# Longer slots for matmul operands, and one work slot fewer in the attention lane

## The chip, the cores and the metric

The kernel runs on one core of a Trainium2 chip. The metric is the time of one execution on the device in microseconds (us). The profiler records one execution with every instruction of the engines: PE (TensorE's matmuls), PEld (TensorE's weight loads, which run beside the matmuls), DVE (VectorE), ACT (ScalarE), POOL (GpSimd) and SP (SyncE, which issues the transfers here).

## The reference

Two models follow each other on 512 tokens of width 1024. The first has one layer: a mix of gated linear attention, a causal convolution and sliding-window attention, then a feed-forward block of width 2816. The second has two layers, each with attention over the 128 best keys of an index score, a gated recurrence, and a feed-forward block. Cut to the parts that this change touches:

```python
u = rmsnorm(h, g_ffn)                                   # first model
hid = causal_dwconv(u @ w_up, ffn_conv_w)
h = h + (silu(hid[..., :2816]) * hid[..., 2816:]) @ w_down
...
for l in range(2):                                      # second model
    proj = rmsnorm_2(x, norm_mix[l]) @ w_in[l]
    aq, ak, av, iq, ik, iw, hq, hf, hi, hg, ga, gb = split(proj)
    aq, ak = rope(norm(aq)), rope(norm(ak))
    y_attn = dsa_attention(aq, ak, av, rope(iq), rope(ik), iw)   # softmax over top 128 keys
    y_hgrn = norm(hgrn2(hq, hf, hi)) * silu(hg)
    x = x + (sigmoid(ga) * (y_attn @ w_a[l]) + sigmoid(gb) * (y_hgrn @ w_h[l])) @ w_out[l]
    g, u = split(rmsnorm_2(x, norm_ffn[l]) @ w_ffn_in[l])
    x = x + (silu(g) * u) @ w_ffn_out[l]
```

All values are 32-bit floats, and the kernel keeps about that precision.

## The kernel before

Activations lie transposed: eight tiles `h` of 128 features by 512 tokens. Every large product is made of matmuls with a moving operand of 128x512 and a stationary operand of 128x128. To keep precision, each operand is split into a rounded part and a remainder (`xh` and `xl`, `whi` and `wlo`, `acth` and `actl`), and each pair of tiles is multiplied three times: wlo·xh, whi·xl, whi·xh (lines 193 to 195 in `project`). One projection over the model width is eight steps of three matmuls into one bank of the accumulation memory; a down-projection of the feed-forward block has 22 steps. In `project_tokens` (lines 168 to 170) the roles are swapped: 128 columns of `xh` or `xl` are stationary and the weight tile moves, over four token blocks.

`weights` issues the transfer of a raw weight tile from SP (512 KB, one of three `wraw` buffers), lets ACT copy four 128x128 pieces at a time into `whi` and lets DVE or POOL subtract them for `wlo`. There are three `whi` and three `wlo` buffers.

A pool hands out slots. The weight pool holds `wraw`, `whi`, `wlo`; the activation pool holds eight `xh` and eight `xl` (`make_x`); the work pool has the lanes `t` (32 slots: split outputs `acth`, `actl`, `mgh`, `mgl`, the mixes' outputs `yah`, `yhh`, `ych`, `ysh`, `ygh` and their remainders, and other longer-lived tiles), `i` (8), `g` (5), `h` (7, short-lived work of the recurrence and feed-forward) and `a` (7, short-lived work of the attention). Each slot has 512 elements per partition, 2048 bytes. In the built program the slots lie one behind the other, and the first addresses are 54,240 for `whi`, 60,384 for `wlo`, 66,528 for `xh`, 82,912 for `xl` (all 32 above a multiple of 64, and 480 above one of 512) and 115,712 for lane `t` (a multiple of 512).

A scheduler decides the order of instructions on each engine; it knows how many slots each lane has. Each engine then works its list in that order. In a layer of the second model, lane `a` is used by index rotation (`rope`, lines 791 to 794, into `idxr`), score selection (`rel`; DVE's 16 rounds of `max` and `match_replace`, lines 878 and 879), key and query rotation (`rotated`: `rope` into `aro`, a multiplication by the norm on DVE at line 817, four transposes on TensorE at line 239) and attention itself (`aL`, `aPT`, `aon`).

Of the kernel before, what the change touches and what calls it, by code (L numbers as in the profile page):

```python
# [10 lines left out]
F32 = mybir.dt.float32  # L11
F32R = mybir.dt.float32r
# [6 lines left out]
P = 128  # L19
T = 512  # L20
NT = 4
KD = 8
# [26 lines left out]
def constants():  # L49
    c = np.zeros((P, NCST), np.float32)  # L50

    def put(name, a):
        c[:, CST[name][0]:CST[name][1]] = a

    i = np.arange(P)[:, None]
    j = np.arange(P)[None, :]
    put("ident", i == j)
    put("inv", np.float32(10000.0) ** (-np.arange(0, 64, 2, dtype=np.float32) / np.float32(64)))
    k = np.arange(2 * P)[None, :]
    dist = P + i - k  # L60
    put("dist", np.where((dist >= 0) & (dist < P), -dist, NEG))
    put("causal", np.where(j <= i, 0.0, NEG))
    put("unseen", np.where(j <= i, 0.0, UNSEEN))
    m = [(i <= j) & (i // 64 == j // 64), i == j]
    for h in LEVELS:
        n = np.repeat(np.arange(64 // h), h)[None, :]
        m.append((i // (2 * h) == n) & (i % (2 * h) < h))
    return c, np.concatenate(m, axis=1).astype(np.float32)


class Builder:
    def __init__(self, ctx, tc, A):
# [13 lines left out]
        self.mixing()  # L86
        self.pending = None

    def t(self, name, dtype=F32, shape=None):
        return self.bp.tile(shape or [P, T], dtype, name=name, tag="t", bufs=self.SLOTS["t"])  # L90

    SLOTS = {"t": 32, "i": 8, "g": 5, "h": 7, "a": 7}
    BANKS = {"h": 2, "a": 2}

    @contextmanager
# [9 lines left out]
        self.lows = [self.nc.vector]  # L105

    def i(self, name, dtype=F32, shape=None):
        return self.bp.tile(shape or [P, T], dtype, name=name, tag="i", bufs=self.SLOTS["i"])

    def g(self, name, dtype=F32, shape=None):  # L110
        return self.bp.tile(shape or [P, T], dtype, name=name, tag="g", bufs=self.SLOTS["g"])

    def u(self, name, dtype=F32, shape=None):
        return self.bp.tile(shape or [P, T], dtype, name=name, tag="u" + self.lane, bufs=self.SLOTS[self.lane])

# [17 lines left out]
    def weights(self, src, n, w=P, pieces=False):  # L133
        nc = self.nc
        ws = []
        step = 512 // w if w < 512 // 2 else 1
        with self.tc.high_priority():
            raw = self.wp.tile([P, 1024], F32, name="wraw", tag="wraw", bufs=3)[:, 0:n * w].rearrange(
                "p (n w) -> p n w", n=n)
            if pieces:  # L140
                for k in range(n):
                    nc.sync.dma_start(raw[:, k, :], src[:, k, :])
            else:
                nc.sync.dma_start(raw, src)
            for k in range(0, n, step):
                m = min(step, n - k)
                wh, wl = [self.wp.tile([P, 512], F32R, name=a, tag=a, bufs=3)[:, 0:m * w].rearrange(
                    "p (m w) -> p m w", m=m) for a in ("whi", "wlo")]
                nc.scalar.copy(wh, raw[:, k:k + m, :])  # L149
                eng = self.lows[self.count % len(self.lows)]  # L150
                self.count += 1
                eng.tensor_tensor(wl, raw[:, k:k + m, :], wh.bitcast(F32), op=OP.subtract)  # L152
                ws += [(wh[:, i, :], wl[:, i, :]) for i in range(m)]
        return ws

    def project_tokens(self, src, X, out):
        nc = self.nc
        w = src.shape[-1]
        ps = [self.mm() for _ in range(NT)]
        for k in range(0, KD, 2):  # L160
            if k == KD - 2 and self.finish:
                self.finish()
                self.finish = None
            ws = self.first.pop(0) if self.first else self.weights(src[k // 2], 2, w)
            for i, (wh, wl) in zip((k, k + 1), ws):
                for t in range(NT):
                    xh, xl = [x[:, t * P:(t + 1) * P] for x in X[i]]
                    nc.tensor.matmul(ps[t][:, 0:w], xh, wl, start=i == 0, stop=False)  # L168
                    nc.tensor.matmul(ps[t][:, 0:w], xl, wh, start=False, stop=False)  # L169
                    nc.tensor.matmul(ps[t][:, 0:w], xh, wh, start=False, stop=i == KD - 1)  # L170
                    if i == KD - 1:
                        with self.tc.high_priority():
                            out(t, ps[t][:, 0:w], self.rcol[:, t:t + 1])

    def token_copies(self, src, X, name):
        tiles = [self.t(name) for _ in range(NT)]

        def out(t, ps, r):
            self.nc.scalar.activation(tiles[t][:, 0:ps.shape[1]], ps, AF.Copy, scale=r)

        self.project_tokens(src, X, out)
        return tiles
# [53 lines left out]
    def transpose4(self, src, dst, idx=None):  # L236
        ps = self.at([P, NT, P])
        for t in range(NT):
            self.nc.tensor.transpose(ps[:, t, :], src[:, t * P:(t + 1) * P], self.ident)  # L239
        if dst is not None:  # L240
            self.nc.scalar.copy(dst, ps)
        return ps
# [32 lines left out]

    def make_x(self, d, h, g):
        nc = self.nc
        hi = self.xp.tile([P, T], F32R, name="xh", tag="xh", bufs=KD)
        lo = self.xp.tile([P, T], F32R, name="xl", tag="xl", bufs=KD)
        nc.scalar.activation(hi, h, AF.Copy, scale=g)  # L280
        nc.vector.scalar_tensor_tensor(lo, h, g, hi.bitcast(F32), op0=OP.mult, op1=OP.subtract)  # L281
        return hi, lo
# [814 lines left out]
```

## Time and profile before

| | |
|---|---|
| runs | 2606.26, 2607.33, 2609.94 us |
| median | 2607.33 us |
| profiled execution, first to last instruction (span) | 2605.2 us; the profile gives no other time of it |
| TensorE matmuls | busy 2533.9 us, 97% of the span |
| DVE, ACT, POOL | 52%, 38%, 29% |

The span of the profiled execution is 2.1 us under the median of the runs. An engine is busy in a group for as long as at least one of the group's instructions is in flight; successive matmuls overlap in time, so the sum of their durations is more than the busy time, and the rate is read from the distance between starts.

### The profile page before, as it was taken

How to read it: one execution, taken by the hardware profiler on the slowest of the kernel's cores; microseconds unless marked ns; L12 is line 12 of the kernel's file. 1: busy time of each engine (PE TensorE's matmuls, PEld its weight loads, DVE VectorE, ACT ScalarE, POOL GpSimd, SP SyncE). 2: the span in 40 equal slices, each digit the busy share in tenths (PEclk: the TensorE clock that was granted, in tenths of full speed). 3: DMA queues.
4: the chain of work that ended last, by engine and by line, in shares of the span. 5: the costliest groups of instructions: out<-in, count | busy, mean ns of one | idle time of the engine just before them, and what ended most of it. 6: DMA issues, size and time to landing. Idle time of an engine off the chain costs nothing.

```text
span 2605.2 us, 31523 instructions
## 1 busy us (share of the span) xinstructions
PE 2533.9 (97%) x11742; PEld 2040.0 (78%) x11742; DVE 1355.5 (52%) x2568; ACT 1000.8 (38%) x1813; POOL 754.3 (29%) x640
## 2 busy tenths in 40 slices
PE   9999999999999997999999999999799999999999
PEld 7777888788888865777878888887577787888887
DVE  4565322477774579675244444336967524444432
ACT  5543333444443333553343333334354433433321
POOL 4234334511101234443351111013545435211100
PEclk9999999999999999999999999999899999999999
DMA  3112222222222221111322222322110122222232
GB/s 135 57 51 81 93 94 93 101 97 96 97 94 90 90 73 65 42 41 51 99 96 94 97 95 94 96 88 81 65 49 33 45 94 97 97 97 97 95 101 87
DMA packets 67434, 217.66 MB, mean 84 GB/s; under 512 B 7744, under 2 KB 8640, under 8 KB 67280
## 3 DMA queue, kind: packets, MB, share of 16 engines
q1 hardware_dynamic: 67280, 215.65, 24.9%
q8 instruction: 92, 1.51, 0.2%
q14 instruction: 62, 0.51, 0.1%
HBM read 213.52 MB, written 2.10 MB: 83 GB/s over the span
## 4 chain that ended last, share of the span: by engine, by line
PE 83%; DVE 12%; issue 2%; POOL 2%; ACT 1%; DMA 0%; SPq 0%; DVEq 0%; POOLq 0%; ACTq 0%
PE mm L194 24%; PE mm L195 24%; PE mm L193 24%; PE at L917 1%; PE mm L169 1%; PE mm L168 1%; PE mm L170 1%; DVE score L879 1%; PE at L929 1%; DVE m L878 1%; DVE wlo L152 1%; PE at L239 1%; DVE hf L490 1%; DVE rope L792 1%; DVE rsq_w L232 1%
## 5 line engine op out<-in xcount | busy, mean ns | idle before, releaser
L149 ACT CAST whi<-wraw 128x512 fp32r<-128x512 f32 (+3 forms) x824 | 502.2, 610 | 1177.7 <-PE mm L195 992.1
L194 PE MATMUL mm<-xl,whi 128*128 128x512 f32 x1920 | 757.2, 394 | 0.0
L193 PE MATMUL mm<-xh,wlo 128*128 128x512 f32 x1920 | 756.8, 394 | 0.0
L195 PE MATMUL mm<-xh,whi 128*128 128x512 f32 x1920 | 755.5, 393 | 0.0
L152 DVE TENSOR_TENSOR wlo<-wraw,whi 128x512 fp32r<-128x512 f32 (+1 forms) x529 | 387.4, 732 | 457.9 <-ACT whi L149 455.2
L152 POOL TENSOR_TENSOR wlo<-wraw,whi 128x512 fp32r<-128x512 f32 (+2 forms) x295 | 383.6, 1301 | 767.0 <-ACT whi L149 747.1
L194 PEld LDWEIGHTS mm<-xl,whi 128*128 128x128 f32 x1920 | 361.7, 188 | 79.8 <-issue 7.5
L195 PEld LDWEIGHTS mm<-xh,whi 128*128 128x128 f32 x1920 | 361.6, 188 | 78.2 <-issue 5.6
L193 PEld LDWEIGHTS mm<-xh,wlo 128*128 128x128 f32 x1920 | 361.5, 188 | 76.6 <-issue 3.5
L193 PE MATMUL mm<-acth,wlo 128*128 128x512 f32 x528 | 208.6, 395 | 0.0
L195 PE MATMUL mm<-acth,whi 128*128 128x512 f32 x528 | 208.6, 395 | 0.0
L194 PE MATMUL mm<-actl,whi 128*128 128x512 f32 x528 | 208.6, 395 | 0.0
L725 POOL TENSOR_TENSOR fg<-fg,rstd 128x512 f32<-128x512 f32 x44 | 56.7, 1289 | 426.1 <-ACT fg L724 426.1
L168 PE MATMUL mm<-wlo,xh 128*128 128x512 f32 (+2 forms) x384 | 146.6, 382 | 20.0 <-POOL wlo L152 12.4
L170 PE MATMUL mm<-whi,xh 128*128 128x512 f32 (+2 forms) x384 | 144.5, 378 | 0.0
L169 PE MATMUL mm<-whi,xl 128*128 128x512 f32 (+2 forms) x384 | 144.2, 375 | 0.2 <-DVE xl L281 0.2
L202 DVE TENSOR_TENSOR gate<-mm,rstd 128x512 f32<-128x512 f32 x56 | 38.7, 691 | 169.3 <-PE mm L195 169.3
L270 POOL TENSOR_TENSOR acc<-acc,sq 128x512 f32<-128x512 f32 x39 | 58.7, 1506 | 205.9 <-ACT sq L267 204.9
L195 PEld LDWEIGHTS mm<-acth,whi 128*128 128x128 f32 x528 | 99.0, 187 | 24.3
L193 PEld LDWEIGHTS mm<-acth,wlo 128*128 128x128 f32 x528 | 99.0, 187 | 24.2
L194 PEld LDWEIGHTS mm<-actl,whi 128*128 128x128 f32 x528 | 99.0, 187 | 24.2
L168 PEld LDWEIGHTS mm<-wlo,xh 128*128 128x128 f32 x384 | 73.5, 191 | 40.7 <-POOL wlo L152 15.7
(347 smaller groups left out, 3288.3 us busy)
## 6 DMA issues: line engine op xcount, KB each, us to landing
wraw<-in_w_ffn_in SPq DMA_DIRECT2D x88, 512.0 KB, 3.2
wraw<-in_w_gate SPq DMA_DIRECT2D x56, 512.0 KB, 3.2
wraw<-in_w_in SPq DMA_DIRECT2D x52, 512.0 KB, 3.2
wraw<-in_w_up SPq DMA_DIRECT2D x44, 512.0 KB, 3.2
wraw<-in_w_tok SPq DMA_DIRECT2D x32, 512.0 KB, 3.2
wraw<-in_w_ffn_out SPq DMA_DIRECT2D x32, 512.0 KB, 3.5
wraw<-in_w_down SPq DMA_DIRECT2D x16, 512.0 KB, 3.5
wraw<-in_w_po SPq DMA_DIRECT2D x32, 256.0 KB, 2.6
```

The costliest lines, as they stand in the source:

```text
L149: nc.scalar.copy(wh, raw[:, k:k + m, :])
L152: eng.tensor_tensor(wl, raw[:, k:k + m, :], wh.bitcast(F32), op=OP.subtract)
L168: nc.tensor.matmul(ps[t][:, 0:w], xh, wl, start=i == 0, stop=False)
L169: nc.tensor.matmul(ps[t][:, 0:w], xl, wh, start=False, stop=False)
L170: nc.tensor.matmul(ps[t][:, 0:w], xh, wh, start=False, stop=i == KD - 1)
L193: nc.tensor.matmul(ps, wl, xh, start=i == 0, stop=False)
L194: nc.tensor.matmul(ps, wh, xl, start=False, stop=False)
L195: nc.tensor.matmul(ps, wh, xh, start=False, stop=i == n - 1)
L202: self.nc.vector.tensor_tensor(out, ps, other, op=OP.mult)
L232: nc.vector.scalar_tensor_tensor(w, w, -0.5, y, op0=OP.mult, op1=OP.mult)
L270: (nc.vector if d % 2 and len(acc) > 1 else nc.gpsimd).tensor_tensor(a, a, sq, op=OP.add)
L725: nc.gpsimd.tensor_tensor(g, g, self.rstd, op=OP.mult)
```

## The change

Three kinds of buffer become 8 elements, 32 bytes, longer: the work lanes `t`, `i` and `g`, the split weights `whi` and `wlo`, and the split activations `xh` and `xl`. Each tile still uses its first 512 elements. The raw weights, the lanes `h` and `a`, and everything else keep their size. Lane `a` has 6 slots, not 7.

```diff
+    PAD = 8
+
+    def padded(self, pool, name, tag, bufs, dtype=F32, shape=None):
+        a = pool.tile([P, T + self.PAD], dtype, name=name, tag=tag, bufs=bufs)
+        if shape is None:
+            return a[:, 0:T]
+        n = math.prod(shape[1:])
+        if len(shape) == 2:
+            return a[:, 0:n]
+        return a[:, 0:n].rearrange("p (n c) -> p n c", n=shape[1])
+
     def t(self, name, dtype=F32, shape=None):
-        return self.bp.tile(shape or [P, T], dtype, name=name, tag="t", bufs=self.SLOTS["t"])
-
-    SLOTS = {"t": 32, "i": 8, "g": 5, "h": 7, "a": 7}
+        return self.padded(self.bp, name, "t", self.SLOTS["t"], dtype, shape)
+
+    SLOTS = {"t": 32, "i": 8, "g": 5, "h": 7, "a": 6}
...
     def i(self, name, dtype=F32, shape=None):
-        return self.bp.tile(shape or [P, T], dtype, name=name, tag="i", bufs=self.SLOTS["i"])
+        return self.padded(self.bp, name, "i", self.SLOTS["i"], dtype, shape)
 
     def g(self, name, dtype=F32, shape=None):
-        return self.bp.tile(shape or [P, T], dtype, name=name, tag="g", bufs=self.SLOTS["g"])
+        return self.padded(self.bp, name, "g", self.SLOTS["g"], dtype, shape)
...
-                wh, wl = [self.wp.tile([P, 512], F32R, name=a, tag=a, bufs=3)[:, 0:m * w].rearrange(
+                wh, wl = [self.wp.tile([P, 512 + self.PAD], F32R, name=a, tag=a, bufs=3)[:, 0:m * w].rearrange(
...
-        hi = self.xp.tile([P, T], F32R, name="xh", tag="xh", bufs=KD)
-        lo = self.xp.tile([P, T], F32R, name="xl", tag="xl", bufs=KD)
+        hi = self.padded(self.xp, "xh", "xh", KD, F32R)
+        lo = self.padded(self.xp, "xl", "xl", KD, F32R)
```

The addresses in the built program (bytes in each partition; the remainder to 64 in brackets):

| buffer | before | after |
|---|---|---|
| whi | 54240 (32), 56288 (32), 58336 (32) | 54240 (32), 56320 (0), 58400 (32) |
| wlo | 60384 (32), 62432 (32), 64480 (32) | 60480 (0), 62560 (32), 64640 (0) |
| xh | 66528 (32), 68576 (32), ... 80864 (32) | 66720 (32), 68800 (0), ... 81280 (0) |
| xl | 82912 (32), 84960 (32), ... 97248 (32) | 83360 (32), 85440 (0), ... 97920 (0) |
| lane t | 115712 (0), 117760 (0), 119808 (0), ... | 116416 (0), 118496 (32), 120576 (0), ... |

The instructions and their order are the same outside of three places in the attention lane of each layer of the second model; the matmuls of the projections keep their order throughout. The largest of the three places is key rotation. On TensorE, during the token projection of the queries (`whi`, `wlo` against `xh`, `xl`), the four transposes of each rotated key block (`at<-csts,aro`) stood like this before:

```order
L168 MATMUL mm<-wlo,xh 128x512
L169 MATMUL mm<-whi,xl 128x512
L170 MATMUL mm<-whi,xh 128x512
L239 MATMUL at<-csts,aro 128x128 x4
L168 MATMUL mm<-wlo,xh 128x512
L169 MATMUL mm<-whi,xl 128x512
L170 MATMUL mm<-whi,xh 128x512
L239 MATMUL at<-csts,aro 128x128 x4
L168 MATMUL mm<-wlo,xh 128x512
L169 MATMUL mm<-whi,xl 128x512
L239 MATMUL at<-csts,aro 128x128 x4
```

and now:

```order
L181 MATMUL mm<-whi,xh 128x512
L179 MATMUL mm<-wlo,xh 128x512
L180 MATMUL mm<-whi,xl 128x512
L250 MATMUL at<-csts,aro 128x128 x4
L181 MATMUL mm<-whi,xh 128x512
L179 MATMUL mm<-wlo,xh 128x512
L180 MATMUL mm<-whi,xl 128x512
L250 MATMUL at<-csts,aro 128x128 x4
L181 MATMUL mm<-whi,xh 128x512
L179 MATMUL mm<-wlo,xh 128x512
L250 MATMUL at<-csts,aro 128x128 x4
```

The first group of transposes has moved behind two more matmuls; the fourth group, which came three matmuls after the third, now comes fourteen after it. On DVE, in the same place, the norm's multiplication of the rotated keys (`aro<-aro,rsq_y`) stood between the rounds of score selection (`MAX`, `MATCH_REPLACE`) and the last rope product (`rope_8001`) like this before:

```order
L793 TENSOR_TENSOR rope_8001<-akx,tabS 128x8x32
L879 MATCH_REPLACE score<-m_7686,score 128x384
L233 SCALAR_TENSOR_TENSOR rsq_y<-rsq_w,rsq_y 128x32
L878 MAX m_7689<-score 128x8
L817 TENSOR_TENSOR aro<-aro,rsq_y 128x512
L879 MATCH_REPLACE score<-m_7689,score 128x384
L817 TENSOR_TENSOR aro<-aro,rsq_y 128x512
L878 MAX m_7692<-score 128x8
L817 TENSOR_TENSOR aro<-aro,rsq_y 128x512
L879 MATCH_REPLACE score<-m_7692,score 128x384
L817 TENSOR_TENSOR aro<-aro,rsq_y 128x512
```

and now:

```order
L889 MAX m_7689<-score 128x8
L244 SCALAR_TENSOR_TENSOR rsq_y<-rsq_w,rsq_y 128x32
L804 TENSOR_TENSOR rope_8001<-akx,tabS 128x8x32
L890 MATCH_REPLACE score<-m_7689,score 128x384
L828 TENSOR_TENSOR aro<-aro,rsq_y 128x512
L889 MAX m_7692<-score 128x8
L828 TENSOR_TENSOR aro<-aro,rsq_y 128x512
L890 MATCH_REPLACE score<-m_7692,score 128x384
L828 TENSOR_TENSOR aro<-aro,rsq_y 128x512
L889 MAX m_7695<-score 128x8
L889 MAX m_7721<-score 128x8
```

The first multiplication now stands behind the match-replace of `m_7689`, and the fourth has moved out of these rows, with six instructions between it and the third.

## Rows read from the trace of the kernel before

**Rows 1.** The page: busy time by engine, and the chain that ended last.
```profile
PE 2533.9 (97%) x11742; PEld 2040.0 (78%) x11742; DVE 1355.5 (52%) x2568; ACT 1000.8 (38%) x1813; POOL 754.3 (29%) x640
...
PE 83%; DVE 12%; issue 2%; POOL 2%; ACT 1%; DMA 0%; SPq 0%; DVEq 0%; POOLq 0%; ACTq 0%
```

**Rows 2.** Groups of PE's matmuls by form: count | busy us, mean ns | idle before.
```profile
L194 PE MATMUL mm<-xl,whi 128*128 128x512 f32 x1920 | 757.2, 394 | 0.0
...
L193 PE MATMUL mm<-acth,wlo 128*128 128x512 f32 x528 | 208.6, 395 | 0.0
...
L168 PE MATMUL mm<-wlo,xh 128*128 128x512 f32 x288 | 117.4, 408 | 20.0 <-POOL wlo L152 12.4 <-DVE wlo L152 4.5 <-ACT lbe L775 2.0
...
L194 PE MATMUL mm<-mgl,whi 128*128 128x512 f32 x192 | 76.2, 397 | 0.7 <-DVE mgl L212 0.7
```

**Rows 3.** Timeline of PE in an up-projection, eleven successive matmuls: start us, duration us.
```profile
1409.06 0.39 PE L194 MATMUL mm<-xl,whi 128*128 128x512 f32 x1
...
1411.33 0.39 PE L195 MATMUL mm<-xh,whi 128*128 128x512 f32 x1
```

**Rows 4.** Windows: an up-projection, a down-projection; busy us and (count), PEclk.
```profile
1409.00:1609.00 200.00, 200.00 (x884) 165.58 (x884) 87.54 (x129) 68.58 (x110) 24.49 (x19) 1.00 0.28 98
...
2498.00:2598.00 100.00, 100.00 (x431) 80.30 (x430) 28.36 (x44) 22.13 (x38) 0.00 (x0) 1.00 0.33 98
```

**Rows 5.** Timeline of PE in a merge, twelve matmuls from the first on yhh.
```profile
1320.41 0.40 PE L193 MATMUL mm<-yhh,wlo 128*128 128x512 f32 x1
...
1321.11 0.40 PE L193 MATMUL mm<-yhh,wlo 128*128 128x512 f32 x1
...
1322.98 0.40 PE L195 MATMUL mm<-yhh,whi 128*128 128x512 f32 x1
```

**Rows 6.** Timeline of PE in a merge, twelve matmuls from the first on xh after ych.
```profile
343.18 0.40 PE L193 MATMUL mm<-xh,wlo 128*128 128x512 f32 x1
...
343.88 0.40 PE L193 MATMUL mm<-xh,wlo 128*128 128x512 f32 x1
...
344.80 0.39 PE L194 MATMUL mm<-xl,whi 128*128 128x512 f32 x1
...
345.71 0.39 PE L195 MATMUL mm<-xh,whi 128*128 128x512 f32 x1
```

**Rows 7.** Groups of PEld's weight loads in the two windows of rows 4.
```profile
L194 PEld LDWEIGHTS mm<-xl,whi 128*128 128x128 f32 x295 | 55.4, 188 | 11.6
...
L195 PEld LDWEIGHTS mm<-acth,whi 128*128 128x128 f32 x144 | 27.0, 187 | 6.6
```

**Rows 8.** ACT's costliest group, the copy into whi.
```profile
L149 ACT CAST whi<-wraw 128x512 fp32r<-128x512 f32 (+3 forms) x824 | 502.2, 610 | 1177.7 <-PE mm L195 992.1 <-PE mm L170 142.4 <-issue 30.6
```

**Rows 9.** Timeline of all engines at key rotation, first layer of the second model.
```profile
984.30 1.26 POOL L794 TENSOR_TENSOR aro<-rope,rope 128x512 f32<-128x512 f32 x1 [1.33 <-DVE rope L793]
...
985.53 1.53 DVE L792 TENSOR_TENSOR rope<-akx,tabS 128x256 f32<-128x256 f32 x1
...
990.41 1.32 DVE L817 TENSOR_TENSOR aro<-aro,rsq_y 128x512 f32<-128x512 f32 x1
...
991.65 0.08 DVE L879 MATCH_VALUE_LOAD score<-m,score 128x8 f32 x1
991.73 0.54 DVE L879 MATCH_REPLACE8 score<-m,score 128x384 f32<-128x384 f32 x1
...
991.79 1.11 PE L239 MATMUL at<-csts,aro 128*128 128x128 f32 x4 [8.35 <-DVE aro L817]
```

**Rows 10.** Timeline of all engines at index rotation, second layer of the second model.
```profile
1769.86 0.31 DVE L792 TENSOR_TENSOR rope<-idx,sin 128x160 f32<-128x160 f32 x1
...
1770.08 0.87 POOL L794 TENSOR_TENSOR idxr<-rope,rope 128x320 f32<-128x320 f32 x1 [0.56 <-DVE rope L793]
```

**Rows 11.** Timeline of PE in the index's token projection, ten successive matmuls.
```profile
902.23 0.31 PE L169 MATMUL mm<-whi,xl 128*128 128x324 f32 x1
...
903.57 0.31 PE L169 MATMUL mm<-whi,xl 128*128 128x324 f32 x1
```

## Prediction

> **What bounds the kernel now.** I read the busy shares and the chain of waits first, to see which engine is the bound; then the costliest groups, for what that engine does; then its timeline in single matmuls, because this change touches no instruction of the main stream and can only act through how long each one takes. TensorE is busy 97% of the span and holds 83% of the chain that ended last [rows 1]. Nearly all of it is one form, a moving operand of 128x512 against a stationary 128x128 [rows 2]. So the number that matters is the step, from the start of one such matmul to the start of the next.
>
> There are two kinds of step in this trace. Where the moving operand is a normed activation (`xh`, `xl`), starts lie 2.27 us apart over ten steps, 227 ns each [rows 3]; over a whole window it is (200.00 + 0.389) us / 884 = 226.7 ns [rows 4] (a matmul lasts 389 ns, so the window counts that much more). Where the moving operand is a work-pool tile (`acth`, `actl`, also `mg` and the `y`s), it is (100.00 + 0.395) us / 431 = 232.9 ns [rows 4]. The engine is busy for the whole of both windows and its granted clock is 1.00, the higher level, in both [rows 4], so nothing upstream and no throttle makes the difference of some 6 ns. The weight load takes 188 and 187 ns [rows 7], so it isn't that either.
>
> The layout offers a reason. In the program before, every `whi`, `wlo`, `xh` and `xl` slot starts 32 bytes past a multiple of 64, and every work-pool tile starts on a multiple of 64, because all slots are 2048 bytes. The fast step has moving and stationary operand at the same offset, the slow one has them 32 bytes apart. The trace can't separate that from "the moving operand's own offset counts", nor from another difference between the two kinds of tile. The switch between kinds is immediate one way and slow the other. Into `yhh` the first three steps take 0.70 us, 233 ns each, and the eleven steps to 1322.98 take 2.57 us, 233.6 ns each [rows 5]. Out of `ych` into `xh` the first three again take 0.70 us, and the first seven 1.62 us, 231 ns each; the four after them take 0.91 us, 227 ns [rows 6]. So the fast step looks like a settled rhythm of two streams, one that is reached only after about seven matmuls at constant offsets.
>
> **The change part by part.**
>
> *The pad.* A slot becomes 2080 bytes, so offsets alternate 32, 0, 32, ... from slot to slot in all these pools. In one projection, `xh` and `xl` of step k now sit at 32 for even k and 0 for odd k, and `whi` and `wlo` of one load sit at opposite offsets. Same and different offsets then come about half and half: counted over the changed program, 4735 of the 9456 wide matmuls have the moving operand at 0, against 2832 before, in runs of three; the relation to the next weight load changes after one to three matmuls almost everywhere. If the settled rhythm needs seven matmuls at constant offsets [rows 6], it is never reached. What a step costs when offsets keep changing isn't in the trace; the nearest rows are the steps just after a switch. The low bound is 231 ns (seven steps out of `ych` [rows 6]), the high one 234 ns (the steps in `yhh`, rounded up [rows 5]). I take 232.5, between them, as the alternation is quicker than a seven-step transition but half of it is in the good relation.
>
> The sum: of the 9456, 6624 have moving or stationary `x` tiles that sit in the good relation today (1920 x 3 with moving `x`, and 288 x 3 of the token projections, where `x` is stationary [rows 2]); some 600 of these already come just after a stall or a switch and gain or lose little. So 6000 x (232.5 - 226.7) ns = +34.8 us. The other 2832 (528 x 3 on `act` and 192 x 3 on `mg` [rows 2], and 224 x 3 on the `y`s, from the loops: seven branches of eight projections with four steps) go from 233.4 (between 232.9 and 233.6, nearer the second as the merges step so too) to 232.5, -2.5 us [rows 4, 5]. Bounds by the same count: at 231 ns, +25.8 - 6.8 = +19 us; at 234 ns, +43.8 + 1.7 = +45 us.
>
> The writers of these buffers (the copies that make `whi`, the subtractions that make `wlo`) may also get faster or slower. That costs nothing while they stay hidden: ACT's `whi` copy is busy 502.2 us and idle 1177.7 us before its instructions, 992.1 us of it waiting for TensorE to free a buffer [rows 8]. A copy of 610 ns would have to nearly triple before TensorE waits for it.
>
> *One slot fewer in the attention lane.* I laid the tiles that share a slot in the changed program over the times of before. Nearly all handovers keep over 1 us of room. The tight ones are rope tiles: key rotation's last one starts at 985.53 and would take over a tile that POOL reads until 984.30 + 1.26 = 985.56 [rows 9]; index rotation in the second layer starts at 1769.86 and would wait until POOL is done at 1770.08 + 0.87 = 1770.95, 1.1 us [rows 10]. Attention's own tiles keep their order on every engine. The scheduler answers by moving rotation work: on DVE the first multiplication of `aro` falls behind one more match-replace, 0.54 + 0.08 us [rows 9]. TensorE stands 8.35 us waiting for exactly this product [rows 9], with the next projection's matmuls queued behind the transposes, so the delay is on the path; but two matmuls, 0.46 us, now stand ahead of the transposes and fill part of it. The fourth product comes some 3 us later on DVE, and its transposes come 14 matmuls, 3.2 us, after the third's, so no new wait. Per second-mix layer +0.1 to +0.6 us, and index rotation up to 1.1 us once: 0 to +2 us, taken as +0.6.
>
> Together +34.8 - 2.5 + 0.6 = +33 us. On the profiled execution that is 2605.2 + 33 = 2638 us of span; the median of the runs shown is 2607.3, 2.1 above that span, so about 2640 us.
>
> **The rivals.**
>
> *Every matmul simply takes the time of its own offsets, without memory.* Then half are fast: 4735 - 2832 = 1903 more slow ones at 6.7 ns (233.4 - 226.7), +12.7 us, and with the slot 2620 us. For it: the first step into `yhh` is slow at once [rows 5]. Against it: seven slow steps at good offsets [rows 6].
>
> *The offset is not the cause.* The two kinds of tile differ in pool and in distance too, and then the pad does nothing: 2607 to 2609 us. The Trainium skill, page "SBUF — State Buffer", section "Who interferes with whom", says as much by its rule: TensorE has two independent read ports, one for the moving operand and one for weight loads, and never waits for anyone. By that rule the pad is worth 0 us, and two ports of one engine would not disturb each other. What speaks against this rival is that one form has two steps, at one clock and without idle time, and that they change within a few matmuls of a change of tile [rows 5, 6].
>
> *Faster: the streams collide today, and spreading parts them.* Before, all differences between moving and stationary start are 0 or 32 bytes from a multiple of 512; after, all sixteen multiples of 32 occur about equally often. If most of these are free of collisions, the step falls to what the columns alone cost. With 324 columns nine steps take 1.34 us, 148.9 ns [rows 11]; so 188 columns cost 226.7 - 148.9 = 77.8 ns, 512 cost 212 ns, and some 15 ns don't depend on columns. All of it away is 9456 x 14.8 ns = -140 us, 2467 us; half of it, 2537 us; it decides from the point where a quarter of it is saved (33 of 140). The Trainium skill, page "TensorE: Matmul & The Clock Gate", section "Back-to-back issue gap", gives N/2.4 + 2.5, 215.8 ns at 512 columns, for an isolated stream; by that figure, an estimate, the full gain would be some -103 us. Against this rival: no run of steps under 226.7 stands in any row, though the unsettled steps drift through many alignments, and a 512-byte weight tile is read across all of these positions anyway, wherever it begins.
>
> **How the numbers follow.** Rhythm lost (2640, its own range 2625 to 2655): 0.47. Half and half (2620): 0.23. Pad without effect (2608): 0.14. Faster (2460 to 2595): 0.16. A measurement of this kernel tells about 0.2%, 5 us, from no change. So slower 0.70, same 0.14, faster 0.16. The range keeps the first three, with 5 us above and 3 below them for the unknown costs: 2604 to 2660.
>
> **What would show it.** In windows of the up-projections the count of matmuls in 200 us should fall from 884 to about 862, and their mean duration rise from 389 towards 395 ns; in the down-projection the 232.9 ns should hardly move. Equal counts in both, near 871, mean half and half. Counts unchanged mean the offset was never the cause; 890 or more in either mean that collisions were parted. The wait for `aro` should stay near 8.4 us per layer. The prediction is wrong if some of the new offsets are better than both of the old ones, which no row can show.

## The result, and the profile after

The changed kernel takes 2634.7 us (median of 4 runs, 2633.3 to 2636.3) where the kernel before takes 2607.4: 1.0103 times as long, 95% interval 1.0089 to 1.0117. It is slower by 27 us; forecast were 33 us and 2640 us. Its profiled span is 2634.5 us, 29.3 more than before. Line numbers after the new helper are 11 higher: the three matmuls of `project` are lines 204 to 206, the transposes line 250, `aro` line 828.

The page of the changed kernel, busy time by engine and the chain that ended last, answers to [rows 1]:

```profile
PE 2562.6 (97%) x11742; PEld 2044.0 (78%) x11742; DVE 1357.1 (52%) x2568; ACT 998.9 (38%) x1813; POOL 754.1 (29%) x640
...
PE 82%; DVE 13%; issue 2%; POOL 2%; ACT 1%; DMA 0%; SPq 0%; DVEq 0%; POOLq 0%; ACTq 0%
```

TensorE is busy for 28.7 us more with the same 11742 matmuls; DVE, ACT and POOL work as long as before within 2 us. So nearly all of the loss is in how long the matmuls take. The page's costliest groups, count | busy us, mean ns | idle before, answer to [rows 2]:

```profile
L205 PE MATMUL mm<-xl,whi 128*128 128x512 f32 x1920 | 766.9, 399 | 0.0
...
L205 PE MATMUL mm<-actl,whi 128*128 128x512 f32 x528 | 208.4, 395 | 0.0
```

The group on `x` is longer by 5 ns in each matmul, the one on `act` isn't. Windows of the changed kernel in an up-projection and in the last down-projection (busy us and count by engine, then the granted clock) answer to [rows 4]:

```profile
1430.00:1630.00 200.00, 200.00 (x864) 161.81 (x863) 85.57 (x127) 67.28 (x108) 23.25 (x18) 1.00 0.28 95
2526.00:2626.00 100.00, 100.00 (x433) 81.03 (x432) 29.04 (x45) 22.68 (x39) 0.00 (x0) 1.00 0.35 103
```

By the same working as there, the step on `x` is (200.00 + 0.393) us / 864 = 231.9 ns, where it was 226.7, and the step on work slots (100.00 + 0.395) us / 433 = 231.9, where it was 232.9. The clock is 1.00 in both and TensorE never idles. The timeline of PE shows the same in single matmuls, eleven successive ones, ten steps in 2.32 us [rows 3]:

```profile
1433.64 0.40 PE L205 MATMUL mm<-xl,whi 128*128 128x512 f32 x1
...
1435.96 0.40 PE L206 MATMUL mm<-xh,whi 128*128 128x512 f32 x1
```

A window's count is uncertain by one, 0.3 ns in 200 us and 0.5 ns in 100 us. Below, a step is therefore also given as the mean distance between starts over all successive wide matmuls of one kind in the trace, leaving out distances of 250 ns and more (stalls and stretches at the lower clock, 254 to 280 of 9226): some 5370 with `x` moving, 2820 with a work slot moving, 765 of the token projections. By this measure the kernel before has 227.3, 233.4 and 227.9 ns and the changed one 232.1, 232.0 and 231.8. Of the trace's 29.3 us these steps are 5370 x 4.77 + 765 x 3.85 - 2820 x 1.39 = 25.6 + 2.9 - 3.9 = +24.6 us; 4.7 us are left for the slot and all else.

The waits of PE in the changed kernel (us in total, times, longest):

```profile
PE at L250 <- DVE aro L828: 17.3, 8, 7.3
...
PE at L936 <- ACT aL L932: 4.1, 2, 2.0
```

and the same two in the kernel before:

```profile
PE at L239 <- DVE aro L817: 20.0, 8, 8.4
...
PE at L925 <- ACT aL L921: 1.5, 2, 0.8
```

The second has grown; the experiment on the slot shows where that comes from.

### The profile page after: what moved, and what is told of

Read it like the earlier page. It is cut to its first block, busy times and chain, and to the rows that moved or that the text cites. A ratio compares the mean times of both kernels' runs of the same rounds, so it can differ in the third digit from the quotient of the medians.

```text
span 2634.5 us, 31537 instructions
## 1 busy us (share of the span) xinstructions
PE 2562.6 (97%) x11742; PEld 2044.0 (78%) x11742; DVE 1357.1 (52%) x2568; ACT 998.9 (38%) x1813; POOL 754.1 (29%) x640
## 4 chain that ended last, share of the span: by engine, by line
PE 82%; DVE 13%; issue 2%; POOL 2%; ACT 1%; DMA 0%; SPq 0%; DVEq 0%; POOLq 0%; ACTq 0%
PE mm L205 24%; PE mm L206 24%; PE mm L204 24%; DVE score L890 2%; DVE m L889 1%; PE at L928 1%; PE at L940 1%; PE mm L181 1%; PE mm L180 1%; PE mm L179 1%; DVE wlo L163 1%; PE at L250 1%; DVE rope L803 1%; DVE hf L501 1%; DVE acc L695 1%
## 5 line engine op out<-in xcount | busy, mean ns | idle before, releaser
L205 PE MATMUL mm<-xl,whi 128*128 128x512 f32 x1920 | 766.9, 399 | 0.0
L206 PE MATMUL mm<-xh,whi 128*128 128x512 f32 x1920 | 764.2, 398 | 0.0
```

What stands on the lines that cost most here:

```text
L205: nc.tensor.matmul(ps, wh, xl, start=False, stop=False)
L206: nc.tensor.matmul(ps, wh, xh, start=False, stop=i == n - 1)
```

## The experiments

Two things were to be settled: whether the operands' positions set the step at all, and by which rule; and what the slot is worth. "Relation" below means the start of the moving operand less the start of the stationary one, in bytes; "to 256 bytes" means the remainder after division by 256.

**The slot alone.**

```diff
-    SLOTS = {"t": 32, "i": 8, "g": 5, "h": 7, "a": 7}
+    SLOTS = {"t": 32, "i": 8, "g": 5, "h": 7, "a": 6}
```

> The kernel before with one slot fewer in the attention lane and no pad. The theory (the pad makes the loss by mixing offsets, the slot costs 0 to 2 us): 2607 to 2610 us, 884 matmuls in the window 1409 to 1609 us. The rival (the slot's new order and waits make the loss): about 2634 us, with the extra 27 us as idle time of TensorE at key rotation and in attention.

Measured: 2613.1 us, ratio 1.0021 (1.0011 to 1.0030), +5.7 us, above the 0 to 2 us that I expected and far below the rival's 27. The steps are those of before (227.3 and 233.4 ns), as is the window of an up-projection:

```profile
1430.00:1630.00 200.00, 200.00 (x884) 165.49 (x883) 88.77 (x130) 69.11 (x111) 23.23 (x18) 1.00 0.29 97
```

Matching each wide matmul's start with the same one before, the trace loses 2.9 us by 1080 us, 1.8 around index rotation of the second layer, and 2.5 around its attention. The waits of PE, as above:

```profile
PE at L239 <- DVE aro L817: 16.9, 8, 7.3
...
PE at L925 <- ACT aL L921: 4.2, 2, 2.1
```

The wait that I had costed, for `aro`, grew shorter (16.9 us in all, 20.0 before). In its place TensorE waits 2.1 us for the first softmax tile `aL` of each layer. The timeline of ACT at this place, with the slot gone (the time in brackets is idle time and what ended it):

```profile
1037.51 1.28 ACT L921 ACT_TABLE_LOAD   x1 [2.99 <-DVE anm L919]
1038.81 0.40 ACT L921 ACTIVATE aL<-aL,anm 128x128 f32<-128x128 f32 x1
```

and the same in the kernel before:

```profile
1034.37 1.28 ACT L921 ACT_TABLE_LOAD   x1
1037.30 0.40 ACT L921 ACTIVATE aL<-aL,anm 128x128 f32<-128x128 f32 x1 [1.64 <-DVE anm L919]
```

Before, ACT loads the table for the exponential early and then stands waiting for the row maximum `anm`; the load is hidden. With six slots `aL` takes over a slot that POOL used last, so in the built program the activation has two engines to wait for. The wait for DVE is then an instruction of its own and stands ahead of the table load. The load comes after the wait, 1.28 us late, and TensorE's wait for `aL` grows from 0.77 to 2.11 us. That happens once per layer, so it accounts for 2.7 us.

The 1.8 us around index rotation of the second layer are for the most part the granted clock. TensorE waits there for `wlo`, 2.82 us with the slot gone and 2.59 before. The eight steps behind this wait then take 3.46 us at a granted 0.50, the lower level of 1.2 GHz, where before they took 1.95 us at 1.00. The windows, first with the slot gone and then before:

```profile
1777.80:1781.00 3.20, 3.20 (x8) 2.52 (x9) 1.69 (x1) 0.00 (x0) 1.15 (x1) 0.50 0.61 191
...
1774.40:1776.10 1.70, 1.70 (x8) 1.40 (x9) 1.68 (x1) 0.00 (x0) 1.13 (x1) 1.00 0.46 123
```

This part is not shown to be the slot's: the kernel with equal positions below keeps seven slots, waits 2.59 us at the same place, and has 0.50 there too (1763.5 to 1766.5 us). Some 3 us at 0.50 or 0.51 also follow each of the two waits for `aL` with the slot gone, but follow neither of them in the kernel of the lanes alone, which has six slots as well. So one trace does not settle how the 5.7 us divide beyond the 2.7.

**Same remainder to 64, at 32 and at 0.** In the first kernel the work pool starts 32 bytes later, so that all operands start 32 above a multiple of 64; in the second the residual pool does too, so that all start on a multiple of 64 (the first added line is in the second kernel only).

```diff
         self.hp = pool("resid", bufs=1)
+        self.hp.tile([P, 8], F32, name="shift0")
...
         self.bp = pool("work", bufs=1)
+        self.bp.tile([P, 8], F32, name="shift", tag="shift", bufs=1)
```

> The kernel before with the work pool moved by 32 bytes, so that every operand of the wide matmuls starts 32 bytes past a multiple of 64; sizes, slots and order are as before. The theory (a step is fast when moving and stationary operand have the same offset within 64 bytes, for long enough): the 2832 steps on work-pool tiles fall from 233.4 to 226.7 ns, -19 us, and the slow steps after each change of tile go too, -1 us: 2587 us. The rival (something else about work-pool tiles makes them slow): 2607 us and 233 ns as before.

> The kernel before with weights and split activations moved by 32 bytes, so that every operand of the wide matmuls starts on a multiple of 64. The theory (only the difference of the offsets counts): 2587 us, as with all at 32. The rival (a moving operand that starts on a multiple of 64 is slow by itself): all steps at 233.4 ns, 6000 x 6.7 ns = +40 us, 2647 us.

Measured: 2596.78 and 2596.75 us, both 0.9957 of before (0.994 to 0.997), -10.7 us where -20 was expected. Windows of the first kernel, as above:

```profile
1430.00:1630.00 200.00, 200.00 (x884) 165.49 (x883) 86.20 (x127) 67.75 (x109) 22.20 (x18) 1.00 0.30 96
2489.00:2589.00 100.00, 100.00 (x439) 82.04 (x438) 29.29 (x46) 22.73 (x39) 0.00 (x0) 1.00 0.36 105
```

and of the second the down-projection:

```profile
2489.00:2589.00 100.00, 100.00 (x438) 82.05 (x437) 29.04 (x45) 22.73 (x39) 0.00 (x0) 1.00 0.36 105
```

`x` stays at 227.4 ns, work slots go from 233.4 to 229.1 in both. So positions do count, and only relative to each other: moving everything by 32 bytes changes nothing. But 229.1 is not 226.7. To 512 bytes, `x` has the relation 0 here and the work slots have 64: the remainder to 64 is not the whole rule.

**Pads of 64 bytes.** The weights' and `x` slots are 64 bytes longer, not 32, and the lanes not longer, so that every remainder to 64 stays as it was before; lane `a` has six slots (that line of the edit is left out here).

```diff
-                wh, wl = [self.wp.tile([P, 512], F32R, name=a, tag=a, bufs=3)[:, 0:m * w].rearrange(
+                wh, wl = [self.wp.tile([P, 512 + 16], F32R, name=a, tag=a, bufs=3)[:, 0:m * w].rearrange(
-        hi = self.xp.tile([P, T], F32R, name="xh", tag="xh", bufs=KD)
-        lo = self.xp.tile([P, T], F32R, name="xl", tag="xl", bufs=KD)
+        hi = self.xp.tile([P, T + 16], F32R, name="xh", tag="xh", bufs=KD)[:, 0:T]
+        lo = self.xp.tile([P, T + 16], F32R, name="xl", tag="xl", bufs=KD)[:, 0:T]
```

> Slots of whi, wlo, xh and xl are 64 bytes longer, not 32, lane t, i, g as before, attention lane with 6 slots: successive slots lie at successive offsets, but the remainder to 64 stays constant. The theory (the remainder to 64 counts, and alternating it costs the settled rhythm): 2607 to 2610 us, 884 matmuls in the window. Rivals: if spreading over 512 bytes costs by itself, 2620 to 2635 us; if it parts collisions, under 2600 us.

Measured: 2635.2 us, ratio 1.0106 (1.0089 to 1.0122): as slow as the change. Windows:

```profile
1430.00:1630.00 200.00, 200.00 (x862) 161.55 (x861) 85.42 (x125) 67.25 (x108) 23.23 (x18) 1.00 0.28 95
2524.00:2624.00 100.00, 100.00 (x431) 80.70 (x430) 29.06 (x45) 22.16 (x39) 0.00 (x0) 1.00 0.34 100
```

`x` has 232.1 ns although its remainder to 64 always equals that of the weights. My theory that the remainder to 64 decides fell here. Left were two: each relation over a longer distance has its own step and the changed kernel shows a mean (A), or any change of the relation from step to step breaks a rhythm (B).

**Constant relations.** Each of five kernels keeps all slots and puts one tile at the head of the activation pool and one at the head of the work pool (of 0 and 120 elements; 16 and 8, shown here; 48 and 8; 8 and 104; 24 and 8), so that each kind of step keeps one relation throughout.

```diff
         self.xp = pool("acts", bufs=1)
+        self.xp.tile([P, 16], F32, name="shift_xp", tag="shift_xp", bufs=1)
         self.bp = pool("work", bufs=1)
+        self.bp.tile([P, 8], F32, name="shift_bp", tag="shift_bp", bufs=1)
```

> The kernel before with 480 bytes ahead of the work pool, so that the weights, the x buffers and the work slots all start at the same remainder to 512 bytes, and every step of the wide products has the relation that before only the x steps have. Theory A (each relation of the moving operand to the weights, to 512 bytes, has its own step, and the 232 ns of the changed kernel is a mean over relations) and theory B (a constant relation that is a multiple of 64 bytes is quick, and it is the change of the relation from step to step that costs) both give 226.7 ns for the 2832 work-slot steps instead of 233.4: 2832 x 6.7 = -19 us, 2588 us. A theory that the work slots are slow for another reason than their relation leaves 229.1 to 233.4 ns there: 2597 to 2607 us.

> Shifts of 64 bytes ahead of the x buffers and 32 ahead of the work pool: the x steps (6000, and 864 of the token projections with the roles exchanged) keep one relation of 64 bytes, the work-slot steps one of 128 bytes. Both theories: x 229.1 ns, as the work-slot steps showed at 64 bytes, +1.7 x 6864 = about +12 us. Work-slot steps: A, whose mean over relations must come to 232, about 232 ns (-4 us, 2615 us in all); B 227 to 229 ns (-13 to -18 us, 2602 us).

> Shifts of 192 bytes ahead of the x buffers and 32 ahead of the work pool: x steps at a constant 192 bytes, work-slot steps at a constant 256. A: about 232 ns for both, +5 x 6864 = +34 us and -4 us, 2637 us. B: 227 to 229 ns for both, +0 to +14 us and -13 to -18 us, 2590 to 2608 us.

> Shifts of 32 bytes ahead of the x buffers and 416 ahead of the work pool: x steps at a constant 32 bytes, the relation that the work-slot steps had before, and work-slot steps at 480, which is 32 bytes the other way. Both theories: x 233.4 ns if the relation alone counts and not which buffers have it, +6.5 x 6864 = about +43 us. Work-slot steps: 231 to 233.4 ns, -7 to 0 us. About 2646 us. If the work slots were slow for what they are and not for their relation, the x steps stay near 227 ns and the time near 2607 us.

> Shifts of 96 bytes ahead of the x buffers and 32 ahead of the work pool: x steps at a constant 96 bytes, work-slot steps and the token projections at a constant 160, the two relations to 256 bytes that are not yet measured. A (a map of steps, its mean over the eight relations 232.0 as in the changed kernel): 8 x 232.0 less the six known (226.9, 233.3, 229.2, 232.5, 233.3, 233.3) leaves 467.5, some 233.8 ns each: 2608 + 6864 x 6.5 = about 2652 us. B (the change of the relation costs on top): the two lie lower, 229 to 231 ns, so that the mean of the map is below 232: 2608 + 6000 x 2.7 + 864 x 2.7 - 2832 x 3 = about 2618 us.

Measured, in this order: 2590.3 us (ratio 0.9926, 0.9910 to 0.9943), 2617.3 (1.0035), 2622.9 (1.0056), 2642.5 (1.0131), 2641.8 (1.0128). The up-projections of the second and the fifth have 876 and 859 matmuls in the window; the first, the third and the fourth are shown. Windows of the first, with equal positions to 512 bytes:

```profile
1430.00:1630.00 200.00, 200.00 (x884) 165.58 (x884) 86.70 (x128) 67.96 (x110) 21.97 (x17) 1.00 0.28 95
2482.00:2582.00 100.00, 100.00 (x443) 82.81 (x442) 29.67 (x46) 22.83 (x39) 0.00 (x0) 1.00 0.36 106
```

Now the down-projection has the quick step as well: 443 matmuls where before there were 430 or 431. Windows of the third, `x` at 192 and work slots at 256:

```profile
1430.00:1630.00 200.00, 200.00 (x859) 160.29 (x858) 85.01 (x125) 66.28 (x107) 22.75 (x18) 1.00 0.28 93
2512.00:2612.00 100.00, 100.00 (x443) 82.81 (x442) 29.89 (x47) 22.91 (x40) 0.00 (x0) 1.00 0.36 106
```

The two kinds have changed places: `x` is slow, as A had it, and the work slots are quick, as B had it; the time is neither's. And windows of the fourth, `x` at the 32 bytes that the work slots had before:

```profile
1430.00:1630.00 200.00, 200.00 (x858) 160.62 (x858) 85.93 (x126) 66.64 (x107) 22.59 (x18) 1.00 0.28 95
2532.00:2632.00 100.00, 100.00 (x430) 80.54 (x429) 28.45 (x45) 22.06 (x38) 0.00 (x0) 1.00 0.33 98
```

The steps by relation (mean distance of starts, as defined above; "token" are the token projections, where the weights move):

| relation, bytes | ns, and where |
|---|---|
| 0, 256 | 227.1 (x), 226.7 (work, equal positions); 227.0 (work, 256) |
| 32 | 233.3 (x), 233.4 (work, before) |
| 64, 320 | 229.1 (x), 229.1 (work); 229.3 (token, 320) |
| 96 | 233.3 (x), 233.4 (work) |
| 128 | 232.5 (work) |
| 160, 416 | 234.2 (work); 234.2 (token, 416) |
| 192, 448 | 233.3 (x); 233.3 (token, 448) |
| 480 | 233.3 (work), 233.2 (token) |

Whichever buffers have a relation, the step is the same, and in the four pairs of relations that lie 256 bytes apart it is the same too. For 96 and 160 bytes A wanted some 233.8 ns and the trace has 233.3 and 234.2, where B wanted 229 to 231. The mean of the eight (480 stands for 224) is 232.0, just what the changed kernel shows. So far that speaks for A.

**Changing relations.** Two kernels change the relation of `x` from step to step in ways for which A and B differ. The first lengthens the weights' slots by 256 bytes and puts 256 bytes between `xh` and `xl`, with six slots in lane `a`; the second only puts 64 bytes between `xh` and `xl` (its edit is shown; the first has 64 elements there).

```diff
         hi = self.xp.tile([P, T], F32R, name="xh", tag="xh", bufs=KD)
+        if not hasattr(self, "part"):
+            self.part = self.xp.tile([P, 16], F32, name="part", tag="part", bufs=1)
         lo = self.xp.tile([P, T], F32R, name="xl", tag="xl", bufs=KD)
```

> Weight slots 256 bytes longer, 256 bytes between xh and xl, and one slot of the attention lane fewer: the relation of x to the weights changes between 0 and 256 bytes from step to step, and both of these were quick when constant (226.7 and 227.0 ns). A (each relation brings its own step, whatever the one before): x steps stay at 227 ns, work slots at 233.4, and the time is that of the kernel with the slot alone, 2613 us. B (any change of the relation breaks a rhythm): x steps 231 to 232.5 ns, 6864 x 4.7 = +32 us, 2645 us.

> 64 bytes between xh and xl, all slots kept: in each group of three steps two have the relation 0 and one 64 bytes, every time; work-slot steps at a constant 96 bytes. A: x steps (2 x 226.9 + 229.1)/3 = 227.6 ns, the token projections (2 x 226.9 + 233.3)/3 = 229.0 ns, +3 us together; work-slot steps as at 96 bytes in the run of this call that has x there; about 2611 us if these stay near 233.4. B: x steps 231 to 232.5 ns, about +32 us, 2640 us.

Measured: 2615.8 us (ratio 1.0031, 1.0020 to 1.0041), near the slot alone, and 2634.8 us (1.0102, 1.0081 to 1.0122). The up-projection in the first:

```profile
1430.00:1630.00 200.00, 200.00 (x883) 165.46 (x883) 87.75 (x129) 68.22 (x110) 23.23 (x18) 1.00 0.29 95
```

and in the second:

```profile
1430.00:1630.00 200.00, 200.00 (x864) 161.82 (x863) 86.04 (x126) 67.33 (x108) 23.19 (x18) 1.00 0.28 95
```

A change by 256 bytes costs nothing (227.3 ns), so the relation counts to 256 bytes and "any change" in B falls. But with two quick steps out of three at 0 and the third at 64, A wanted 227.6 ns and the trace has 232.0: 231.9 after `xh`, at the best relation, and 232.1 after `xl`. The steps of the changed kernel, sorted by their own relation, say the same: on `x` 232.2 ns at 0, the quickest when constant, and 230.0 at 160, the slowest when constant. A step does not have the time of its own relation alone; a relation that changes by anything but 256 bytes takes the quick step from all three. So A falls as well.

Of B, counted to 256 bytes, this much stands: `x` has its quick step only while the relation stays the same. That every change costs does not stand. With the pads of 64 bytes the work slots change among 32, 96, 160 and 224 bytes and take 232.8 ns, less than the 233.3 to 234.2 of these four when constant. And in the token projections of the second kernel here, where the weights move, the steps differ by their own relation after all: 229.1 ns at 0 and 235.0 at 192, both above their constant 227.9 and 233.3; the mean is 231.1 ns, where A wanted 229.0.

**The lanes alone.** The change without the longer weights' and `x` slots: `t`, `i`, `g` 32 bytes longer, six slots in `a`.

> A part of the change alone: the slots t, i and g 32 bytes longer and one slot of the attention lane fewer; weights and x buffers as before. x steps at 227.3 ns as before; work-slot steps at the mean of the relations, 231.6 to 232 ns, 2832 x -1.6 = -4.5 us; the slot +5.7 us as it measured alone: 2609 us, and the rest of the change's +27 us belongs to the padding of weights and x buffers.

Measured: 2608.7 us, ratio 1.0000 (0.9991 to 1.0009). `x` 227.3 ns, work slots 232.0; windows:

```profile
1430.00:1630.00 200.00, 200.00 (x884) 165.50 (x883) 87.47 (x128) 67.97 (x110) 23.23 (x18) 1.00 0.29 97
2497.00:2597.00 100.00, 100.00 (x433) 81.03 (x432) 29.05 (x45) 22.47 (x39) 0.00 (x0) 1.00 0.34 101
```

This part comes out even: 2820 x 1.34 = 3.8 us won on the steps, and about as much lost by the slot. So the change's 27 us are those of the longer weights' and `x` slots.

## Why the prediction was right, and where not

*The bound and the direction* held. The change acts through TensorE's step and little else; the quick step of `x` is lost, and nothing stands against it.

*The size of the pad.* Forecast were +34.8 us on `x` and -2.5 on the work slots; the steps give +28.5 (25.6 and 2.9 for the token projections) and -3.9. The count was right (6000; 5370 + 765 measured), the difference too large: I charged 226.7 to 232.5, 5.8 ns. Over all quick steps the mean before is 227.3 to 227.9, since it holds the steps after each interruption, and after it is 232.0: 4.7 ns. The step that I chose between 231 and 234 was good to 0.5 ns. The signs named came too: 864 matmuls in the window for "about 862", a duration of 394 ns for "towards 395", and 1 ns of change in the down-projection.

*The reason* was half right. Right were that the relation of the two operands counts, not one's own position, and that the quick step is lost when relations are mixed. Wrong was "the same offset to 64": the relation counts to 256 bytes, and of eight constant relations 32 bytes apart only 0 gives 226.7 ns, 64 gives 229.1, and the other six 232.5 to 234.2. So a constant relation is no guarantee either. That the time came out all the same is in part luck: the step was bounded by rows of unsettled matmuls [rows 5, 6] and not by the rule, and where the rule itself made the forecast, with pads of 64 bytes, it missed by 25 us. Nor does the relation to the next weight load change as soon as I wrote: in the changed program a quarter of the wide matmuls stand in runs of four to six at one remainder to 64, though none in seven. The chance that I gave the rival "half and half" rested on the same 64 bytes. It falls with that: in the changed kernel the steps on `x` at equal remainders to 64 take 231.6 ns, not 226.7.

*That the offset is not the cause* is excluded: moved by 32 bytes, `x` goes from 227.3 to 233.3 ns. The Trainium skill, page "SBUF — State Buffer", section "Who interferes with whom", has the two reads of TensorE independent of each other; the steps here depend on how both operands lie to each other, and the measurement decides.

*Faster by parting collisions* is excluded for this pad: no relation has a step under 226.7 ns. The estimate from the Trainium skill's "TensorE: Matmul & The Clock Gate", section "Back-to-back issue gap", of 215.8 ns, which the page gives for a single isolated matmul, was reached in no run here. Yet the kernel that gives the work slots the relation of `x` is faster than both, 2590.3 us: 18 us under before, 44 under the changed one.

*The slot* was mis-sized: +0.6 us forecast, 0 to 2; +5.7 measured alone. The wait for `aro` was forecast to stay near 8.4 us and fell to 7.3 at its longest; the two more matmuls that stand ahead of it are 0.46 us of that. What I did not see is that a slot's other owner adds a wait to the activation, and that this wait comes ahead of the table load: 2.7 us of the 5.7. I had only asked whether the handover was late; it was not.

The errors of pad and slot have opposite signs and cancel in part, which is luck too: by the trace 24.6 + 4.7 = 29.3 us, against 32.3 + 0.6 = 33.

What stays open: why mixed relations end near 232 ns whatever the mix (232.0 in the changed kernel, with 0 and 64, and in the lanes alone; 232.1 and 232.8 with four relations each; 231.0 and 231.1 in the token projections of the kernels with pads of 64 bytes and with 64 bytes between `xh` and `xl`). That it is also the mean over the eight constant ones is not an explanation, as the mix of 0 and 64 shows. The kernel with 64 bytes between `xh` and `xl` also changes the start of the moving operand from step to step; whether that costs by itself, whatever the relation, no run separates for `x`. What in TensorE's two reads meets is not visible in the trace.

## What to carry to other kernels

Where TensorE is the bound, list the start addresses of moving and stationary operands and try them with equal remainders by 256 across all pools, by a dead tile at the head of a pool and slots that are multiples of 256; here, with operands of 128x512 and 128x128 in 32 bits, 480 dead bytes won 18 us, and no other form was tried. A pad that spreads slots changes the relation of every pair of operands, so count the pairs that lie well today and would be parted as well as those that it would join. When a lane loses a slot, look at more than lateness: look at which instruction gets a second engine to wait for, and what stands behind that wait on its engine.

## What the runs showed of the hardware

The step of a 128x512 matmul in these kernels lies, at a constant relation, between 226.7 and 234.2 ns by addresses alone, at a granted clock of 1.00 in the windows shown; weight loads of `project` have a median of 187 or 188 ns in every run, as in [rows 7]. The sign of the relation counts: 64 bytes ahead take 229.1 ns, 64 behind (448) 233.3. Steps in a slow constant relation aren't even among themselves: at 32 bytes on `x`, 1514 steps of 234 and 1514 of 235 ns, 1115 of 231 and 836 of 233, while the quick one has 227 and 226 in the ratio of two to one, which in whole nanoseconds is an even 226.7. An ACT table load of 1.28 us is hidden or exposed by where a wait stands: TensorE's wait for the first `aL` of a layer was 0.77 us with the load ahead of the wait and 2.11 with the load behind it.
